# DeltaNet mixer: instructions of other engines' results emitted one or more parts later, values first in the chunk stage, and a new layout of the slots

## The chip, the cores and the metric

The kernel runs on one core of one Trainium2 chip. The metric is the device time of one execution in microseconds (us). The core has engines that run side by side, each with its own in-order queue: TensorE (PE; its weight loads are shown as PEld), VectorE (DVE), ScalarE (ACT), GpSimd (POOL) and SyncE (SP), which issues most DMA transfers.

## The reference, cut to what matters

The program is one step of a two-layer network on 128 context and 512 latent tokens of width 1024: a gated DeltaNet mixer, a feed-forward block, a Hyena convolution mixer, a second feed-forward block. The change touches the DeltaNet mixer alone. It has 8 heads with keys and values of 128; tokens are cut into chunks of 64, ten for a head, and each direction (forward, backward) scans its chunks in order:

```python
def step(s, xs):
    w_c, u_c, qd_c, aqk_c, kt_c, gl_c = xs
    v_new = u_c - jnp.einsum('bhcd,bhde->bhce', w_c, s)
    o_c = (jnp.einsum('bhcd,bhde->bhce', qd_c, s)
           + jnp.einsum('bhij,bhje->bhie', aqk_c, v_new))
    s = s * gl_c[..., None, None] + jnp.einsum('bhcd,bhce->bhde', kt_c, v_new)
    return s, o_c
```

Here `w_c` and `u_c` come from triangular systems of each chunk that do not depend on `s`. After the scan, `o` of both directions is summed, RMS-normalised (`o * rsqrt(mean(o*o) + eps)`), multiplied by a gate `silu(h @ w_gate)`, and multiplied by the output weights.

## The kernel before, in words

The mixer's function `gdn` makes one period for each h from -3 to 7. In a period seven kinds of work run for different heads: `gdn_scan(h)`, `gdn_norm(h-1)` (normalise and transpose the output), `gdn_chunks(h+1)`, `gdn_pre(h+2)`, the projections `gdn_gemm(h+3)` and their short convolutions `gdn_conv`, one or two `gdn_gate` products, and some parts of `ada`, which loads and multiplies the modulation weights (128 x 1024 pieces on SyncE's queue). In the last period `gdn_finish` splits the outputs for the output product.

Each of them is a generator whose yields cut it into parts. `weave` hands out the parts over the 30 slots (`SLOTS`) of a period: a stream (generator, n, a, b) has its n parts spread evenly from slot a to slot b; what is left is emitted at the end of the period. The tables `PERIOD`, `GATES` and `LOADS` hold a and b, with three phases for h < 0, h < 5 and the rest; `EMIT` is the order of the streams within a slot. Emission gives the priority; below it a scheduler takes from each engine's ready instructions, so that an engine's final order is near the emitted one but not equal to it.

`gdn_scan` has ten steps for a head, eight on latent chunks in a chain and two on context chunks. One step, for both directions: TensorE multiplies q and k by the state (line 1373, tile `ps_s`), VectorE makes `y` from it with the values `vyz` (L1378), TensorE multiplies by the chunk matrix `lt` (L1384, L1386 where there is no state), ScalarE evicts that to `w` or `od` (L1392), TensorE multiplies by the keys (L1407), VectorE makes the next state `s` (L1413). GpSimd adds the two directions to `o` (L1398), and ScalarE squares a finished token block (L1403, tile `junk`).

`gdn_pre` makes the squared norms (`gdn_norms`: transposes `ps_kq`, squares on ScalarE L1159, then VectorE L1161), the products `ps_kk` and from them `fa` (L1212); writes `fa` to DRAM (`ft`, L1219) and reads its diagonal blocks back as `ln` (L1226), both issued by ScalarE; VectorE negates `ln` to `bn` (L1232, L1233) and inverts small blocks; the result goes through DRAM (`bd`) to the tiles `tm` and `tt`. `gdn_chunks` multiplies these to the chunk matrices: `ps_c` (L1297), `ps_aq` (L1302), three rounds of `ps_y` (L1320) into `lt`, and last transposes the values (`ps_vt`, L1336), which ScalarE evicts in ten pieces to `vyz` (L1341). `ps_vt`, `ps_c`, `ps_aq` and `ps_y` share two PSUM buffers.

Projections, gates and the feed-forward products use three matmuls for one, on high and low parts (`wh`, `wl`, `xh`, `xl`; lines 146 and 134).

Of the kernel before, what the change touches and what calls it, by code (L numbers as in the profile page):

```python
# [35 lines left out]

SLOTS = 30
PERIOD = dict(
    scan=(0, SLOTS),
    norm=(11, 21),  # L40
    pre=((2, 21), (1, 25), (4, 25)),
    chunks=((7, 30), (1, 25), (3, 20)),
    gemm=((2, 8, 14), (0, 10, 20), (22, 0, 11)),
    gemm_len=(8, 7, 10),
    finish=(27, 30),
)
GEMM_ORDER = (1, 0, 2)

GATES = (
    (5, 15, 25),  # L50
    (-3, 17, 20),
    (6, 16, 24),
    (4, 5, 14),
    (4, 13, 28),
    (3, 23, 30),
    (7, 27, 30),
    (7, 3, 15),
)

LOADS = (  # L60
    (0, 0, 28),
    (3, 10, 26),
    (0, 5, 30),
    (10, 3, 26),
    (3, 1, 22),
    (1, 7, 29),
    (3, 6, 30),
    (6, 0, 26),
    (13, 0, 21),
    (18, 0, 24),  # L70
    (11, 5, 30),
)

EMIT = ['scan', 'loads', 'norm', 'conv', 'chunks', 'pre', 'gemm', 'finish', 'gate']
MOD_PARTS = (4, 5, 4, 1, 1, 0, 1, 3, 4)
# [15 lines left out]
class _Kernel:  # L91
# [780 lines left out]
    def gdn(self, xs):  # L872
        nc, A, V, G, PE, I = self.nc, self.A, self.V, self.G, self.PE, self.I
        W = I["gdn_w_in"][0]
        with ExitStack() as st:
# [78 lines left out]
            for h in range(-3, H):  # L954
# [10 lines left out]
                if 0 <= h + 2 < H:  # L965
                    add("pre", self.gdn_pre(h + 2, hd[h + 2]), 18, PERIOD["pre"][ph])
                if 0 <= h + 1 < H:
                    add("chunks", self.gdn_chunks(h + 1, hd[h + 1]), 11, PERIOD["chunks"][ph])
                if 0 <= h + 3 < H:
# [168 lines left out]
    def gdn_norms(self, h, hd):  # L1138
# [7 lines left out]
        for t0, tn in ((0, 2), (2, 2), (4, 1)):  # L1146
            ps = self.pg.tile([128, 512], F32, tag="g", name="ps_kq")
            for n in range(2 * tn):
                t, c = t0 + n // 2, n % 2
                self.PE.transpose(ps[:, n * 128 : n * 128 + 128], qk[:, t, c * 128 : c * 128 + 128],  # L1150
                                  self.ident)
            for c in range(2):
                rs = slice(64 * c, 64 * c + 64)
                A.copy(kz[rs, t0 : t0 + tn, c, :],
                       ps.rearrange("p (t c d) -> p t c d", t=2, c=2)[rs, :tn, c, :])
            for n in range(2 * tn):
                t, c = t0 + n // 2, n % 2
                j = p.tile([128, 128], F32, tag="junk", name="junk")
                A.activation(j, ps[:, n * 128 : n * 128 + 128], AF.Square, accum_out=ss[:, c, t : t + 1])  # L1159
            yield  # L1160
        V.tensor_scalar(out=ss, in0=ss, scalar1=EPS, scalar2=None, op0=ALU.add)  # L1161

# [22 lines left out]
    def gdn_pre(self, h, hd):  # L1185
# [38 lines left out]
        for d in range(2):  # L1224
            src = ft[d * 41600 : (d + 1) * 41600].rearrange("(l x) -> l x", x=1040)[:, :1024]
            nc.scalar.dma_start(ln[64 * d : 64 * d + 40],  # L1226
                                src.rearrange("l (j i) -> l j i", i=64)[:, :, :16])
        yield
        zz, bn = self.zz, self.bn
# [54 lines left out]
    def gdn_chunks(self, h, hd):  # L1284
# [3 lines left out]
        lt = self.lt[h % 2]  # L1288
        fa, tm, tt, rinv, vt = hd["fa"], hd["tm"], hd["tt"], hd["rinv"], hd["vt"]


        for d in range(2):
# [8 lines left out]
            for t in range(NT):  # L1301
                PE.matmul(pa[:, t * 64 : t * 64 + 64], tm[:, d, t, :], fa[:, d, t, 1, :],  # L1302
                          start=True, stop=True)
            view = lambda x: x[:, :320].rearrange("p (t i) -> p t i", t=NT)
            V.tensor_mul(tm[:, d].rearrange("p t (c i) -> p t c i", c=2), _bc(view(pc), 2, 2),
# [6 lines left out]
        for k in range(3):  # L1312
            cur = y if k else tt
            for ds, ts in ((slice(0, 1), slice(0, 4)), (slice(1, 2), slice(0, 4)),
# [16 lines left out]
                yield  # L1331
        vy = self.vyz[h % 2]
        for t0, tn in ((0, 4), (4, 1)):
            pv = pm.tile([128, 512], F32, tag="m", name="ps_vt")
            for t in range(t0, t0 + tn):
                PE.transpose(pv[:, (t - t0) * 128 : (t - t0 + 1) * 128],  # L1336
                             vt[:, t * 128 : (t + 1) * 128], ident)
            for t in range(t0, t0 + tn):
                for c in range(2):
                    rs = slice(64 * c, 64 * c + 64)  # L1340
                    A.activation(vy[rs, t, c, :], pv[rs, (t - t0) * 128 : (t - t0 + 1) * 128], AF.Copy,  # L1341
                                 scale=rinv[rs, c, t : t + 1])
        yield
        hd["vy"] = vy

    def gdn_scan(self, h, hd):
# [7 lines left out]
        seen = {}  # L1354
        state = {}
        for d in range(2):
            s = p.tile([128, 128], F32, tag=f"s1{d}", name="s", bufs=2)
            nc.sync.dma_start(s, self.I["state_delta"][0, 0, d, h])
            state[1, d] = s
# [5 lines left out]
        for pair in steps:  # L1365
# [21 lines left out]
            for seq, d, t, c, rs, ro in pair:  # L1387
# [4 lines left out]
                A.activation(w, pss[d][:, 128:256], AF.Copy, scale=kt[:, c, d, t : t + 1])  # L1392
                seen[t, c] = seen.get((t, c), 0) + 1
            yield
            for seq, d, t, c, rs, ro in pair:
# [3 lines left out]
            for t in {x[2] for x in pair}:  # L1399
                if seen.get((t, 0), 0) + seen.get((t, 1), 0) == 6:  # L1400
                    seen[t, 0] += 1
                    j = p.tile([128, 128], F32, tag="junk", name="junk")
                    A.activation(j, o[:, t, :], AF.Square, accum_out=oss[:, t : t + 1])  # L1403
            if pair[0][:4] == (1, 0, 4, 1):
# [3 lines left out]
            for seq, d, t, c, rs, ro in pair:  # L1408
# [8 lines left out]
                state[seq, d] = s2  # L1417
            yield
        for d in range(2):
            nc.sync.dma_start(self.O[2][0, 0, d, h], state[0, d])  # L1420
# [429 lines left out]
```

## Time and profile before

| | |
|---|---|
| median of 3 runs (lowest to highest) | 2046.1 us (2042.37 to 2047.77) |
| the profiled execution | 2051.41 us, its span 2049.6 us |
| busy in the span: PE, PEld | 1967.1 us (96%), 1818.0 us (89%) |
| busy in the span: DVE, ACT, POOL | 1498.7 us (73%), 949.3 us (46%), 135.5 us (7%) |
| matmuls, DVE and ACT instructions | 13259, 3175, 2185 |
| scans of heads 0 to 7 | from about 270 us to 725 us |

A span of an engine is the time in which at least one of its instructions runs; matmuls are pipelined and overlap, so that a busy PE is not one at its peak. The clock column gives the granted TensorE clock as a share of 2.4 GHz; its lower level is 0.5 (1.2 GHz). The scans of the heads follow each other: head 2 from 376.7 us, head 3 from 431.1, head 4 from 491.1, head 5 from 563.5, head 6 from 621.8, head 7 from 688.0 to 724.9.

### The profile page before, as it was taken

How to read it: one execution, taken by the hardware profiler on the slowest of the kernel's cores; microseconds unless marked ns; L12 is line 12 of the kernel's file. 1: busy time of each engine (PE TensorE's matmuls, PEld its weight loads, DVE VectorE, ACT ScalarE, POOL GpSimd, SP SyncE). 2: the span in 40 equal slices, each digit the busy share in tenths (PEclk: the TensorE clock that was granted, in tenths of full speed). 3: DMA queues.
4: the chain of work that ended last, by engine and by line, in shares of the span. 5: the costliest groups of instructions: out<-in, count | busy, mean ns of one | idle time of the engine just before them, and what ended most of it. 6: DMA issues, size and time to landing. Idle time of an engine off the chain costs nothing.

```text
span 2049.6 us, 34532 instructions
## 1 busy us (share of the span) xinstructions
PE 1967.1 (96%) x13259; PEld 1818.0 (89%) x13259; DVE 1498.7 (73%) x3175; ACT 949.3 (46%) x2185; POOL 135.5 (7%) x241
## 2 busy tenths in 40 slices
PE   7998999999999999999999999999999999999997
PEld 4676888988865789999999998999979999999997
DVE  6887787886663469956956867787787985785674
ACT  4466456655343466533533534333337652452442
POOL 0132011121100100000000000111000000000000
PEclk8999999999998999999999999999999999999999
DMA  7765445343455652223222244222353232232221
GB/s 241 261 203 150 130 113 144 80 116 108 137 167 168 212 181 79 84 74 91 83 73 85 69 129 127 69 88 83 116 172 110 82 92 73 76 92 73 83 59 56
DMA packets 344836, 237.01 MB, mean 116 GB/s; under 512 B 62274, under 2 KB 314810, under 8 KB 344671
## 3 DMA queue, kind: packets, MB, share of 16 engines
q1 hardware_dynamic: 322495, 230.18, 37.6%
q10 hardware_dynamic: 22176, 4.62, 1.1%
q8 instruction: 104, 1.70, 0.3%
q14 instruction: 61, 0.50, 0.1%
HBM read 202.57 MB, written 32.19 MB: 115 GB/s over the span
## 4 chain that ended last, share of the span: by engine, by line
PE 76%; DVE 10%; DMA 5%; ACT 4%; issue 2%; POOL 1%; ACTq 0%; POOLq 0%; DVEq 0%; SPq 0%
PE ps_d L134 15%; PE ps_g L456 11%; PE ps_u L456 11%; PE ps_hp L146 8%; PE ps_o L134 5%; PE ps_gu L456 4%; PE ps_p L146 3%; PE ps_ab L1626 2%; PE ps_ada L212 2%; PE ps_g L1683 2%; DVE cacc L1127 1%; PE ps_gate L146 1%; DMA ln<-ft 1%; PE ps_s L1407 1%; PE ps_y L1320 1%
## 5 line engine op out<-in xcount | busy, mean ns | idle before, releaser
L121 ACT CAST wh<-raw 128x512 fp32r<-128x512 f32 (+2 forms) x241 | 179.0, 763 | 278.0 <-PE ps_d L134 168.3
L122 DVE TENSOR_TENSOR wl<-raw,wh 128x512 fp32r<-128x512 f32 (+2 forms) x241 | 206.8, 873 | 35.5 <-ACT wh L121 34.5
L134 PE MATMUL ps_d<-xh,wh 128*128 128x320 f32 x688 | 212.9, 310 | 3.9 <-ACT wh L121 3.9
L134 PE MATMUL ps_d<-xl,wh 128*128 128x320 f32 x688 | 212.9, 310 | 0.0
L134 PE MATMUL ps_d<-xh,wl 128*128 128x320 f32 x688 | 211.9, 309 | 0.0
L421 ACT CAST ph<-ws 128x512 fp32r<-128x512 f32 x176 | 109.1, 621 | 138.8 <-PE ps_g L456 41.7
L456 PE MATMUL ps_u<-qh,ph 128*128 128x322 f32 x528 | 164.9, 312 | 1.4 <-ACT ps_g L470 1.4
L456 PE MATMUL ps_u<-ql,ph 128*128 128x322 f32 x528 | 165.5, 313 | 0.0
L456 PE MATMUL ps_u<-qh,pl 128*128 128x322 f32 x528 | 163.8, 310 | 0.0
L422 DVE TENSOR_TENSOR pl<-ws,ph 128x512 fp32r<-128x512 f32 x176 | 120.6, 689 | 38.1 <-ACT ph L421 37.6
L572 DVE SCALAR_TENSOR_TENSOR x<-ps_d,ng,x 128x128 f32<-128x128 f32 x144 | 58.7, 435 | 108.9 <-PE ps_d L134 108.9
L134 PEld LDWEIGHTS ps_d<-xh,wh 128*128 128x128 f32 x688 | 129.2, 188 | 5.5 <-ACT wh L121 5.0
L146 PE MATMUL ps_p<-xh,wh 128*128 128x320 f32 x384 | 128.8, 335 | 1.8 <-ACT junk L1159 1.0
L134 PEld LDWEIGHTS ps_d<-xl,wh 128*128 128x128 f32 x688 | 129.2, 188 | 0.8 <-DVE xl L561 0.7
L134 PEld LDWEIGHTS ps_d<-xh,wl 128*128 128x128 f32 x688 | 129.3, 188 | 0.0
L146 PE MATMUL ps_hp<-xh,wh 128*128 128x320 f32 (+1 forms) x384 | 123.6, 323 | 0.7 <-DVE xp L1574 0.7
L146 PE MATMUL ps_p<-xh,wl 128*128 128x320 f32 x384 | 123.0, 320 | 0.0
L146 PE MATMUL ps_p<-xl,wh 128*128 128x320 f32 x384 | 122.8, 320 | 0.0
L146 PE MATMUL ps_hp<-xh,wl 128*128 128x322 f32 (+1 forms) x384 | 120.1, 313 | 0.0
L146 PE MATMUL ps_hp<-xl,wh 128*128 128x320 f32 (+1 forms) x384 | 119.7, 312 | 0.0
L456 PE MATMUL ps_g<-qh,wh 128*128 128x322 f32 x352 | 109.6, 311 | 2.5 <-ACT ps_u L463 2.5
L456 PE MATMUL ps_g<-ql,wh 128*128 128x322 f32 x352 | 110.1, 313 | 0.0
(418 smaller groups left out, 5681.6 us busy)
## 6 DMA issues: line engine op xcount, KB each, us to landing
raw<-in_ada_w_dram SPq DMA_DIRECT2D x96, 512.0 KB
raw<-in_ffn_w_gu_dram SPq DMA_DIRECT2D x88, 512.0 KB
raw<-in_gdn_w_in_dram SPq DMA_DIRECT2D x33, 512.0 KB
raw<-in_ffn_w_down_dram SPq DMA_DIRECT2D x32, 512.0 KB
raw<-in_hy_w_in_dram SPq DMA_DIRECT2D x24, 512.0 KB
h_lat<-hlo SPq DMA_DIRECT2D x16, 512.0 KB
hs<-h_lat SPq DMA_DIRECT2D x32, 256.0 KB
raw<-in_ffn_w_down_dram SPq DMA_DIRECT2D x16, 384.0 KB
```

The costliest lines, as they stand in the source:

```text
L121: self.A.copy(wh[:, ks, :], v[:, ks])
L122: self.V.tensor_sub(wl[:, ks, :], v[:, ks], wh[:, ks, :])
L134: self.PE.matmul(ps, a[:, k, :], b[:, sl], start=(n == 0), stop=(n == 3 * nk - 1))
L146: self.PE.matmul(ps, a[:, k, :], b[:, sl], start=(n == 0), stop=(n == 3 * nk - 1))
L212: PE.matmul(ps[32 * j : 32 * j + 32, :], self.sc[:, k, :], loaded[j * 512 // n][:, c : c + 512], start=(k == 0), stop=(k == KD - 1), skip_ ...
L421: A.copy(h, src)
L422: V.tensor_sub(l, src, h)
L456: self.PE.matmul(ps[:, :322], a[:, k, :], b, start=start and n == 0, stop=n == 11, skip_group_check=True)
L572: V.scalar_tensor_tensor(out=x[d][:, sl], in0=p1[:, pl], scalar=gate[:, c, d : d + 1], in1=x[d][:, sl], op0=ALU.mult, op1=ALU.add)
L1127: V.scalar_tensor_tensor(out=acc[:, c:e], in0=xp[:, k + c : k + e], scalar=wc, in1=acc[:, c:e], op0=ALU.mult, op1=ALU.add)
L1626: PE.matmul(ps, a_[:, m, it, js], b_[it], start=(c == 0), stop=(c == 5))
L1683: PE.matmul(pv[:, gi * 256 : gi * 256 + 256], a_[:, e, cs], b_[:, m, jt, :], start=(c == 0), stop=(c == 11))
```

## The change

The same instructions are emitted, in another order; on each engine their number by line and shape is the same. (1) In `gdn_pre` seven yields (`TRAVEL`) instead of one stand between the load of `ln` and its first reader, and the stream counts 25 parts instead of 18. (2) In `gdn_norms` one yield more stands before VectorE reads the squares. (3) In `gdn_chunks` the transposes and evictions of the values come first instead of last, a yield stands between `ps_c` with `ps_aq` and VectorE's product of `ps_c`, and the stream counts 16 parts instead of 11. (4) In `gdn_scan` the square of a finished block is kept in a list and emitted after the next step's evictions. (5) All slot tables and `EMIT` have new numbers.

```diff
 PERIOD = dict(
     scan=(0, SLOTS),
-    norm=(11, 21),
-    pre=((2, 21), (1, 25), (4, 25)),
-    chunks=((7, 30), (1, 25), (3, 20)),
-    gemm=((2, 8, 14), (0, 10, 20), (22, 0, 11)),
-    gemm_len=(8, 7, 10),
-    finish=(27, 30),
+    norm=(12, 21),
+    pre=((2, 17), (0, 24), (0, 28)),
+    chunks=((7, 29), (3, 21), (3, 20)),
+    gemm=((1, 10, 14), (0, 10, 21), (21, 4, 16)),
+    gemm_len=(3, 7, 4),
+    finish=(26, 27),
 )
 GATES = (
...
-    (4, 5, 14),
+    (2, 12, 13),
...
-    (7, 3, 15),
+    (6, 6, 12),
 )
 LOADS = (
...
-    (13, 0, 21),
+    (16, 1, 21),
...
-    (11, 5, 30),
+    (8, 9, 30),
 )
-EMIT = ['scan', 'loads', 'norm', 'conv', 'chunks', 'pre', 'gemm', 'finish', 'gate']
+EMIT = ['loads', 'finish', 'pre', 'scan', 'conv', 'gemm', 'norm', 'gate', 'chunks']
...
-                    add("pre", self.gdn_pre(h + 2, hd[h + 2]), 18, PERIOD["pre"][ph])
+                    add("pre", self.gdn_pre(h + 2, hd[h + 2]), 18 + TRAVEL, PERIOD["pre"][ph])
-                    add("chunks", self.gdn_chunks(h + 1, hd[h + 1]), 11, PERIOD["chunks"][ph])
+                    add("chunks", self.gdn_chunks(h + 1, hd[h + 1]), 16, PERIOD["chunks"][ph])
...
             yield
+        yield
         V.tensor_scalar(out=ss, in0=ss, scalar1=EPS, scalar2=None, op0=ALU.add)
...
-        yield
+        for _ in range(TRAVEL):
+            yield
         zz, bn = self.zz, self.bn
...
+        vy = self.vyz[h % 2]
+        for t0, tn in ((0, 4), (4, 1)):
+            pv = pm.tile([128, 512], F32, tag="m", name="ps_vt")
+            for t in range(t0, t0 + tn):
+                PE.transpose(pv[:, (t - t0) * 128 : (t - t0 + 1) * 128],
+                             vt[:, t * 128 : (t + 1) * 128], ident)
+            for t in range(t0, t0 + tn):
+                for c in range(2):
+                    rs = slice(64 * c, 64 * c + 64)
+                    A.activation(vy[rs, t, c, :], pv[rs, (t - t0) * 128 : (t - t0 + 1) * 128], AF.Copy,
+                                 scale=rinv[rs, c, t : t + 1])
+        hd["vy"] = vy
+        yield
         for d in range(2):
...
+            yield
             view = lambda x: x[:, :320].rearrange("p (t i) -> p t i", t=NT)
...
-        vy = self.vyz[h % 2]
-        for t0, tn in ((0, 4), (4, 1)):
-            pv = pm.tile([128, 512], F32, tag="m", name="ps_vt")
...
-        yield
-        hd["vy"] = vy
...
+        ripe = []
+        def squares(n):
+            while len(ripe) > n:
+                t = ripe.pop(0)
+                j = p.tile([128, 128], F32, tag="junk", name="junk")
+                A.activation(j, o[:, t, :], AF.Square, accum_out=oss[:, t : t + 1])
...
                 seen[t, c] = seen.get((t, c), 0) + 1
+            squares(0)
             yield
...
-                    A.activation(j, o[:, t, :], AF.Square, accum_out=oss[:, t : t + 1])
+                    ripe.append(t)
...
             yield
+        squares(0)
```

In the changed kernel the line numbers are 2 to 14 higher, and the values' eviction has L1303, their transpose L1298, the square L1367. Three places of the order follow, before and after.

VectorE, period 5: from the products `fa` of the last head (7) to its first reader of `ln`, before:

```order
L1212 TENSOR_TENSOR fa<-ps_kk,X 128x128 x2
L1413 SCALAR_TENSOR_TENSOR s<-s,egl,ps_s 128x128 x2
L1326 TENSOR_TENSOR fa<-tt,ps_y_6752 128x512
L1378 SCALAR_TENSOR_TENSOR y<-ps_s,sy,vyz 128x128 x2
L1326 TENSOR_TENSOR fa<-tt,ps_y_6784 128x512
L1326 TENSOR_TENSOR fa<-tt,ps_y_6822 128x2x128
L1456 TENSOR_TENSOR oT<-oT,gg 128x640
L1413 SCALAR_TENSOR_TENSOR s<-s,egl,ps_s 128x128 x2
L1378 SCALAR_TENSOR_TENSOR y<-ps_s,sy,vyz 128x128 x2
L1330 TENSOR_TENSOR lt<-tt,ps_y_6864 64x4x128
L1232 TENSOR_SCALAR bn<-ln 40x256
```

The same after; the row of `fa` is two rows above the first one here:

```order
L1426 SCALAR_TENSOR_TENSOR s<-s,egl,ps_s 128x128 x2
L228 TENSOR_TENSOR mod_73<-ps_adat,cols_a 128x16 x2
L1391 SCALAR_TENSOR_TENSOR y<-ps_s,sy,vyz 128x128 x2
L1323 TENSOR_TENSOR tm<-ps_c,kg 128x640
L124 TENSOR_TENSOR wl<-raw,wh 128x512
L239 SCALAR_TENSOR_TENSOR acol_8036<-mod_73,cols_a 128x16
L1344 TENSOR_TENSOR fa<-tt,ps_y_6701 128x512
L1426 SCALAR_TENSOR_TENSOR s<-s,egl,ps_s 128x128 x2
L124 TENSOR_TENSOR wl<-raw,wh 128x512
L1391 SCALAR_TENSOR_TENSOR y<-ps_s,sy,vyz 128x128 x2
L1344 TENSOR_TENSOR fa<-tt,ps_y_6733 128x512
L1236 TENSOR_SCALAR bn<-ln 40x256
```

Between `fa` and the reader of `ln` stand 9 rows before and 12 after; the scan's rows `s` and `y` are two pairs of each in both.

ScalarE at the seam from the scan of head 5 to that of head 6, before (the `vyz` are head 6's):

```order
L1403 ACTIVATE junk,oss<-o 128x128
L1341 ACTIVATE vyz<-ps_vt,rinv 64x128
L1403 ACTIVATE junk,oss<-o 128x128
L1341 ACTIVATE vyz<-ps_vt,rinv 64x128 x8
L1392 ACTIVATE od<-ps_s,kt 128x128
L1434 ACTIVATE o<-o,of 128x128 x5
L1392 ACTIVATE od<-ps_s,kt 128x128
```

The same seam after (the `vyz` are head 7's; head 6's stand in the period before):

```order
L1405 ACTIVATE w<-ps_s,kt 128x128 x2
L1303 ACTIVATE vyz<-ps_vt,rinv 64x128 x2
L1405 ACTIVATE w<-ps_s,kt 128x128
L1303 ACTIVATE vyz<-ps_vt,rinv 64x128 x3
L1405 ACTIVATE w<-ps_s,kt 128x128
L1303 ACTIVATE vyz<-ps_vt,rinv 64x128 x2
L1367 ACTIVATE junk,oss<-o 128x128
L1303 ACTIVATE vyz<-ps_vt,rinv 64x128
L1367 ACTIVATE junk,oss<-o 128x128
L1303 ACTIVATE vyz<-ps_vt,rinv 64x128 x2
L1327 COPY tt<-ps_aq 64x5x64 x2
L1448 ACTIVATE o<-o,of 128x128 x5
```

Before, eight pieces stand in a row ahead of the scan's first `od`; after, pieces in twos and threes stand between the last `w` of head 5.

TensorE in the next to last step of head 2's scan, from the state's product (L1373) to the product with `lt` (L1384), before:

```order
L1373 MATMUL ps_s<-s,qk 128x128
L146 MATMUL ps_p<-xh_1273,wl 128x320
L1320 MATMUL ps_y_4770<-fa,tm 128x128 x4
L146 MATMUL ps_p<-xh_1081,wh 128x320
L146 MATMUL ps_p<-xl_1082,wh 128x320
L146 MATMUL ps_p<-xh_1081,wl 128x320
L146 MATMUL ps_p<-xh_1180,wh 128x320
L1320 MATMUL ps_y_4777<-fa,tm 128x128 x2
L1384 MATMUL ps_s<-y,lt 128x128
```

After, from the first state's product (now L1386) of such a step at the end of head 2's scan to the keys' product (now L1420), with L1397 for L1384:

```order
L1386 MATMUL ps_s<-s,qk 128x128
L148 MATMUL ps_p<-xl_1266,wh 128x320
L1386 MATMUL ps_s<-s,qk 128x128
L148 MATMUL ps_p<-xh_1265,wl 128x320
L148 MATMUL ps_p<-xh_1273,wh 128x320
L1397 MATMUL ps_s<-y,lt 128x128
L148 MATMUL ps_p<-xl_1274,wh 128x320
L1397 MATMUL ps_s<-y,lt 128x128
L148 MATMUL ps_p<-xh_1273,wl 128x320
L1420 MATMUL ps_s<-w,ktok 128x128
L1298 MATMUL ps_vt<-ident,vt 128x128 x5
L1420 MATMUL ps_s<-w,ktok 128x128
```

Before, seven rows of other work stand in that link; after, two stand in it and one or two in the next.

## Rows read from the trace of the kernel before

**Rows 1.** Windows, scans of heads 2, 5, 6, 7: length, busy by engine, clock, DMA.

```profile
376.70:431.10 54.40, 53.57 (x439) 48.81 (x440) 45.03 (x124) 29.95 (x100) 10.86 (x23) 1.00 0.31 82
...
563.50:621.80 58.30, 53.66 (x405) 39.59 (x405) 37.41 (x115) 25.91 (x89) 7.03 (x12) 0.97 0.55 162
...
621.80:688.00 66.20, 61.78 (x362) 43.16 (x361) 24.57 (x67) 23.03 (x69) 4.83 (x11) 0.85 0.62 201
...
688.00:724.90 36.90, 36.79 (x243) 28.71 (x243) 18.23 (x54) 17.86 (x53) 6.45 (x11) 1.00 0.67 197
```

**Rows 2.** Windows of heads 2, 5, 6, 7, modulation matmuls alone.

```profile
376.70:431.10 54.40, 2.11 (x10) 0.29 (x10) 0.00 (x0) 1.00 0.31 82
...
563.50:621.80 58.30, 12.77 (x65) 1.78 (x64) 0.59 (x1) 0.97 0.55 162
...
621.80:688.00 66.20, 16.47 (x54) 2.10 (x54) 0.59 (x1) 0.85 0.62 201
...
688.00:724.90 36.90, 7.38 (x32) 1.02 (x32) 0.59 (x1) 1.00 0.67 197
```

**Rows 3.** Waits, 176 to 746 us: who waited for whom, total, times, longest.

```profile
ACT junk L1403 <- POOL o L1398: 28.8, 20, 2.7
...
PEld ps_s L1407 <- ACT od L1392: 6.9, 10, 1.7
...
DVE y L1378 <- ACT vyz L1341: 6.5, 6, 1.5
...
DVE bn L1233 <- DMA ln<-ft: 5.6, 5, 2.2
...
PEld ps_s L1407 <- ACT w L1392: 3.0, 12, 0.8
...
DVE bn L1232 <- DMA ln<-ft: 2.8, 3, 1.2
```

**Rows 4.** Timeline, 604 to 609 us: start, duration, engine, line [idle before].

```profile
604.20 0.28 DVE L1232 TENSOR_SCALAR bn<-ln 40x256 f32<-40x256 f32 x1 [1.16 <-DMA ln<-ft]
...
604.37 0.30 PE L146 MATMUL ps_gate<-xh,wh 128*128 128x320 f32 x1
...
604.52 0.30 PE L146 MATMUL ps_gate<-xl,wh 128*128 128x320 f32 x1
...
606.69 0.37 DVE L1233 TENSOR_SCALAR bn<-ln 40x256 f32<-40x256 f32 x1 [2.21 <-DMA ln<-ft]
...
608.51 0.49 PE L1373 MATMUL ps_s<-s,qk 128*128 128x128 f32 x2 [3.69 <-DVE s L1413]
```

**Rows 5.** Windows around the two stalls: columns as in rows 1.

```profile
608.00:612.00 4.00, 3.49 (x18) 3.50 (x19) 3.51 (x17) 0.92 (x3) 0.91 (x2) 0.71 0.00 0
...
612.00:616.00 4.00, 4.00 (x30) 3.91 (x29) 3.25 (x8) 1.42 (x6) 0.20 (x1) 0.87 0.16 63
...
624.00:628.00 4.00, 1.90 (x16) 1.34 (x18) 1.88 (x11) 3.89 (x12) 0.00 (x0) 0.84 0.97 273
...
627.30:647.20 19.90, 19.49 (x88) 13.66 (x88) 3.65 (x8) 4.82 (x14) 0.00 (x0) 0.50 0.45 161
```

**Rows 6.** Timeline, 623 to 627 us, ScalarE and TensorE.

```profile
623.59 3.01 ACT L1341 ACTIVATE vyz<-ps_vt,rinv 64x128 f32<-64x128 f32 x8
...
624.40 0.49 PE L1384 MATMUL ps_s<-y,lt 128*128 128x128 f32 x2 [1.28 <-DVE y L1378]
...
626.62 0.37 ACT L1392 ACTIVATE od<-ps_s,kt 128x128 f32<-128x128 f32 x1
```

**Rows 7.** Timeline, 435 to 437 us, seam to head 3.

```profile
435.78 0.80 PE L1297 MATMUL ps_c<-tm,fa 64*64 64x64 f32 x20 [0.89 <-ACT vyz L1341]
...
436.52 0.35 DVE L1378 SCALAR_TENSOR_TENSOR y<-ps_s,sy,vyz 128x128 f32<-128x128 f32 x1 [1.34 <-ACT vyz L1341]
```

**Rows 8.** Timeline, 715 to 719 us, one scan step of head 7.

```profile
714.97 0.61 PE L1373 MATMUL ps_s<-s,qk 128*128 128x128 f32 x4
...
718.23 0.65 PE L1373 MATMUL ps_s<-s,qk 128*128 128x128 f32 x4
```

More of the change, by code (lines that the diff above doesn't have):

```diff
@@ L37 @@
 SLOTS = 30
+TRAVEL = 7
 PERIOD = dict(
     scan=(0, SLOTS),
-    norm=(11, 21),
-    pre=((2, 21), (1, 25), (4, 25)),
-    chunks=((7, 30), (1, 25), (3, 20)),
-    gemm=((2, 8, 14), (0, 10, 20), (22, 0, 11)),
-    gemm_len=(8, 7, 10),
-    finish=(27, 30),
+    norm=(12, 21),
[4 more added lines that the diff above has]
+    finish=(26, 27),
 )
@@ L49 @@
 GATES = (
-    (5, 15, 25),
-    (-3, 17, 20),
-    (6, 16, 24),
-    (4, 5, 14),
-    (4, 13, 28),
-    (3, 23, 30),
-    (7, 27, 30),
-    (7, 3, 15),
+    (5, 11, 27),
+    (-3, 18, 20),
+    (6, 14, 30),
+    (2, 12, 13),
+    (4, 15, 29),
+    (3, 29, 30),
+    (7, 25, 30),
+    (6, 6, 12),
 )
 LOADS = (
[L61 to L68, printed above, removed]
-    (13, 0, 21),
-    (18, 0, 24),
-    (11, 5, 30),
+    (0, 0, 25),
+    (4, 6, 30),
+    (0, 9, 30),
+    (10, 2, 25),
+    (3, 8, 19),
+    (1, 0, 26),
+    (2, 2, 25),
+    (6, 3, 26),
+    (16, 1, 21),
+    (18, 0, 25),
+    (8, 9, 30),
 )
-EMIT = ['scan', 'loads', 'norm', 'conv', 'chunks', 'pre', 'gemm', 'finish', 'gate']
+EMIT = ['loads', 'finish', 'pre', 'scan', 'conv', 'gemm', 'norm', 'gate', 'chunks']
 MOD_PARTS = (4, 5, 4, 1, 1, 0, 1, 3, 4)
@@ L1331, in gdn_chunks @@
                 yield
-        vy = self.vyz[h % 2]
-        for t0, tn in ((0, 4), (4, 1)):
-            pv = pm.tile([128, 512], F32, tag="m", name="ps_vt")
[L1335 to L1342, printed above, removed]
-        yield
-        hd["vy"] = vy
     def gdn_scan(self, h, hd):
@@ L1401, in gdn_scan @@
                     seen[t, 0] += 1
-                    j = p.tile([128, 128], F32, tag="junk", name="junk")
-                    A.activation(j, o[:, t, :], AF.Square, accum_out=oss[:, t : t + 1])
+                    ripe.append(t)
             if pair[0][:4] == (1, 0, 4, 1):
```

## Prediction

> **What bounds the kernel now.** I began with the busy time by stretch, one stretch for each head's scan, since the change touches only the loop over heads. In [rows 1] the matmul columns are nearly full everywhere, but those spans overlap. The weight loads are the better measure of what the array is fed. Their idle time, the stretch less their busy time, is 5.6 us for head 2, 18.7 for head 5, 23.0 for head 6 and 8.2 for head 7. Part of that is no idleness: the modulation matmuls stream long after a short weight load. Taking their matmul time less their weight-load time off [rows 2], there remain 5.6 - 1.8 = 3.8 us (head 2), 18.7 - 11.0 = 7.7 (head 5) and 23.0 - 14.4 = 8.6 (head 6); these are lower bounds, since the modulation spans overlap others. So TensorE bounds heads 0 to 4 with a few us lost in each, and in heads 5 and 6, where there are no projections left to fill in, the scan's chain from TensorE to VectorE to TensorE to ScalarE and back sets the time. I then looked for what ends the waits [rows 3] and followed the two largest on the timeline.
>
> First, at 604.52 us TensorE starts a gate matmul and then nothing until 608.51 [rows 4]. It needs the new state s from VectorE, and that stands in VectorE's queue behind two negations which wait 1.16 and 2.21 us for the table `ln` to land. Just after it the granted clock is 0.71 and 0.87 [rows 5], so part of the time it is at 1.2 GHz. Second, at the seam from head 5 to 6, ScalarE evicts eight pieces of `vyz` in a row from 623.59 for 3.01 us; TensorE waits 1.28 us for y, which waited for `vyz`, and the scan's own eviction of `od` starts only at 626.62 [rows 6]. The stretch from 624 holds 1.90 us of matmul in 4, and then the clock is 0.50 for 19.9 us [rows 5].
>
> **The change part by part.** No instruction is added or taken away; every gain or loss is a wait.
>
> *(a) TRAVEL.* The first reader of `ln` is emitted seven parts after its load instead of one. In [rows 4] the gap is 608.51 - 604.52 = 3.99 us; two matmuls of that kind start 0.15 us apart, so 3.8 us were lost. At half clock were (1 - 0.71) x 4 / 0.5 = 2.3 and (1 - 0.87) x 4 / 0.5 = 1.0 us, 3.4 in all; with the loads busy for 7.4 of those 8 us it cost half of that by 7.4/8, 1.6 us. Together 5.3 us. The other waits for `ln` are 5.6 + 2.8 - 3.4 = 5.0 us of VectorE [rows 3], and what TensorE lost by them lies between 0 and 5.0. But the order of VectorE for the last head has two scan steps between `fa` and `ln` before, and two after: more rows, not more steps. The transfer itself is unchanged. I take -4, bounds -10.3 and 0.
>
> *(b) Values first in the chunk stage, at the seam of head 6.* The ten evictions of head 6's `vyz` no longer stand between its chunk stage and its scan: y of the first step finds them ready. Lost were 4.00 - 1.90 = 2.1 us, and the half clock over 19.9 us with loads busy for 13.66, which at 2.4 GHz would have been 6.8 us less if nothing else held the scan: 8.9 us. What moves in: head 7's `vyz` now stand at the same seam, but between the last evictions of scan 5, in twos and threes. A wait for an eviction is then one to three pieces long instead of eight. I take -7, bounds -8.9 and 0.
>
> By the Trainium skill (TensorE: Matmul & The Clock Gate, section HAM oscillation — how this bites in real kernels) the penalty is the throttled time by the share of the clock that is lost, here half: 10.0 us instead of my 6.8. The rows show loads busy for only two thirds of that stretch, so I keep mine; by the rule the sum would be 3 us lower.
>
> *(c) The same at the five other seams.* At the seam to head 3 TensorE waits 0.89 us for `vyz` and y 1.34 [rows 7]. All such waits of y come to 6.5 us [rows 3]. One us a seam: -5, bounds -6.5 and 0.
>
> *(d) Squares later.* ScalarE idles 28.8 us in 20 waits for GpSimd's sums [rows 3]. It is not the bound; what TensorE loses is the late eviction behind the square. All of TensorE's weight loads that wait for `od` or `w` lose 6.9 + 3.0 = 9.9 us [rows 3]. The 20 squares stand before at most 20 of 160 evictions, an eighth, though before the later ones: I take twice that share, -2, bounds -9.9 and 0.
>
> *(e) The new slots, at the end of a scan.* One step of three links takes 718.23 - 714.97 = 3.26 us [rows 8], 1.09 each, of which two pairs of matmuls fill about 0.4; the other 0.65 us needs four or five rows of projection at 0.15. In the order a link at the end of head 2's scan had seven such rows and now has one or two. About five such links in each of five heads lack 0.25 us on average, 6 us, where before about half as much was lacking: +3, bounds 0 and +12.
>
> *(f) The new slots, work moved between heads.* Gate 3 (48 matmuls at 0.15, 7.2 us) goes from head 4's period to head 2's; gate 7 goes from head 7's to head 6's; three modulation parts more stand in period 5 and three fewer in 7. Where the scan's chain is the limit the filler is free; where TensorE is, it costs its full time. Above head 2's 3.8 us, heads 5 and 6 idle for 3.9 + 4.8 = 8.7 us, of which (a) and (b) already use 3.8 + 2.1; 2.8 are left. Head 7 idles 8.2 - 6.4 = 1.8 us or more [rows 2]; it is nearly full, so that one gate less may shorten it or bare the chain. -2, bounds one gate either way, -7 and +7. The extra yields after the norms and between `ps_c` and `ps_aq` I cost at nothing: they move a VectorE product behind work that TensorE has queued there, and uncovered would cost the 1 us of one link.
>
> A second rule bears on what is left to gain. By the Trainium skill (Trainium Kernel Development and Optimization, Best Practices) matmul busy time is a poor measure of headroom and weight-load busy time a good one. By matmul busy, head 6's stretch would hold 4.4 us to gain in all, and (b) with (f) could not exceed that; [rows 1] has 23.0 by weight loads, so the trace sides with the rule.
>
> The sum is -4 - 7 - 5 - 2 + 3 - 2 = -17 us. The profiled execution took 2051.4 us (span 2049.6 and 1.8 around it), so 2034.4 for such a one. It lies 5.3 us above the median of the runs, 2046.1; the same 17 us off that median give 2029.
>
> **The rivals.**
> 1. *The clumps only move: no change.* For it: the order still has ten `vyz` in a row in two other places, the same eviction work, and for the last head as many scan steps before `ln`. Against it: y waits for none of them. With (b), (c) and (f) at nothing: 2046.1 - 4 - 2 + 3 = 2043.
> 2. *Starved scan ends: slower.* In periods 0 to 6 the chunk stage ends by slot 21 and the preparation by 24 or 28, so the last steps stand alone with what is left of the projections. If each of the 25 links waits 1.0 us instead of 0.25, that is 25 us, and five stretches at half clock as after [rows 4] lose 1.6 each, 8 us; against the 20 us of gains: 2059. It decides from 0.8 us a link. For it: the thin rows in the order. Against it: in head 7 of before, links as thin run at 1.09 us.
> 3. *The loop levels out: twice the gain.* With (a), (b) and (c) at their good ends, 5 us from the squares and 4 from the moved work, no loss at the ends: 10.3 + 8.9 + 6.5 + 5 + 4 = 35, 2011. For it: head 2 shows that a head can run with 3.8 us idle. Against it: head 5 keeps its slow transfers.
> That the yields do nothing because a scheduler reorders is excluded: `vyz` now stands a whole scan ahead of its user.
>
> **How the numbers follow.** A difference of 0.3%, 2040.0 to 2052.2, is about what this measurement can tell from none. The sum 0.48, rival 3 0.22, rival 1 0.18, rival 2 0.12. Faster is the sum and rival 3, 0.70; same 0.18; slower 0.12. All bounds at their good ends give 2046.1 - 42.6 = 2003.5, at their bad ends 2046.1 + 19 = 2065. The range leaves out most of rival 2: 2003 to 2050; the likeliest alone, 2015 to 2040.
>
> **What the profile after would show.** Right: no TensorE gap near 4 us behind a `bn` negation; waits of y for `vyz` near zero, ScalarE's for GpSimd's sums well under 28.8; the stretch at clock 0.50 in head 6 gone; weight-load idle of heads 5 and 6 several us lower. Wrong: (a), if `bn` still waits 2 us; (b), if the clock falls again in period 6; (e), if the last links idle by a us each. A loss in period 7 of over 5 us would make (f) wrong, and a loss before 237 us, where the preparation of head 0 has nothing beside it, would be one that I have not counted.

## The result and the profile after

The changed kernel takes 2017.0 us (median of 4 runs, 2014.7 to 2017.8) against 2045.2 us (4 runs, 2042.4 to 2047.8): a ratio of 0.9861, 95% interval 0.9844 to 0.9878, 28 us faster. The forecast was 2029, with 2015 to 2040 for its own sum.

The profiled execution after took 2014.7 us, its span 2012.9. It is the lowest of its runs and that of before lies 5 to 6 us above its median, so the two traces differ by 36.7 us, some 8 more than the medians. In the first part of the profile page after, the weight loads are busy for about as long as before (1810.7 us against 1818.0) and the matmuls for 17 us less; so 29 of the 36.7 us are time between weight loads:

```profile
PE 1949.9 (97%) x13259; PEld 1810.7 (90%) x13259; DVE 1501.7 (75%) x3175; ACT 946.4 (47%) x2185; POOL 136.3 (7%) x241
```

The next table is worked out from the traces: the first `ps_s` matmul of head 1, the lengths from each head's first `ps_s` to the next one's, and the length from head 7's to the first `ps_d` matmul, in us (one execution of each kernel; the experiments are told below). `ps_d` is the down product of the feed-forward block behind the mixer; the expectation of e10 calls that point the output product, but the mixer's output product, `ps_o`, starts some 170 to 180 us earlier.

| kernel | head 1 starts | 1 | 2 | 3 | 4 | 5 | 6 | 7 to `ps_d` | `ps_d` starts |
|---|---|---|---|---|---|---|---|---|---|
| before | 316.7 | 60.0 | 54.4 | 60.0 | 72.4 | 58.3 | 66.2 | 207.8 | 895.8 |
| after | 313.9 | 58.8 | 56.4 | 59.6 | 62.5 | 60.0 | 49.7 | 199.1 | 860.0 |
| e1, code alone | 315.9 | 58.0 | 59.6 | 53.6 | 69.9 | 63.1 | 48.9 | 206.6 | 875.6 |
| e9, gates and loads alone | 312.7 | 61.4 | 61.1 | 57.1 | 65.0 | 64.1 | 51.1 | 199.9 | 872.4 |
| e11, values first alone | 317.5 | 60.2 | 57.9 | 62.4 | 72.3 | 60.3 | 52.7 | 207.2 | 890.5 |
| e10, after with the old gates | 316.2 | 60.5 | 59.8 | 55.4 | 69.9 | 60.6 | 45.3 | 205.2 | 872.9 |
| e6, after with the old gates and loads | 321.4 | 62.0 | 57.3 | 59.1 | 69.3 | 60.4 | 50.9 | 208.1 | 888.5 |
| e12, after with gate 4 early | 318.3 | 63.7 | 57.3 | 59.7 | 64.7 | 56.8 | 51.0 | 200.7 | 872.2 |

Of the 36.7 us, 35.8 were gained up to that point: 9.9 in head 4, 16.5 in head 6, 8.7 behind the start of head 7, 2.8 before head 1; heads 2 and 5, which got more filler, are 2 us longer each. The windows of heads 2, 5, 6 and 7 after, against [rows 1]:

```profile
372.70:429.10 56.40, 56.17 (x477) 52.76 (x476) 44.53 (x114) 29.14 (x94) 8.44 (x17) 1.00 0.41 109
551.20:611.20 60.00, 58.44 (x473) 41.15 (x472) 40.40 (x125) 30.53 (x109) 6.43 (x14) 0.99 0.81 246
611.20:660.90 49.70, 49.70 (x351) 39.82 (x349) 21.55 (x55) 15.95 (x50) 4.55 (x10) 0.94 0.65 218
660.90:691.40 30.50, 30.50 (x212) 26.91 (x212) 22.01 (x58) 19.15 (x52) 4.16 (x8) 1.00 0.83 245
```

Weight-load idle fell from 23.0 to 9.9 us in head 6 and from 8.2 to 3.6 in head 7; in head 5 it is 18.9 as before, but the modulation matmuls there [rows 2] grew from 65 to 83 and take 16.74 - 2.44 = 14.3 us of it:

```profile
551.20:611.20 60.00, 16.74 (x83) 2.44 (x82) 0.60 (x1) 0.99 0.81 246
```

Head 4's window, before and then after: the gate that left it is 48 of the 55 matmuls by which x550 became x495, and the length went down by 9.9 us, more than the gate's 7.2.

```profile
491.10:563.50 72.40, 68.70 (x550) 62.66 (x549) 45.80 (x123) 33.83 (x109) 7.54 (x18) 1.00 0.46 133
```

```profile
488.70:551.20 62.50, 60.31 (x495) 54.77 (x494) 42.45 (x118) 30.61 (x102) 8.75 (x14) 1.00 0.46 130
```

The waits after, 176 to 746 us, that answer to [rows 3]; a wait of y for `vyz` has no row any more, and the wait of 2.9 us for `ln` in the last row stands at 245 us, ahead of head 1's scan:

```profile
ACT junk L1367 <- POOL o L1412: 19.7, 17, 3.5
...
PEld ps_s L1420 <- ACT w L1405: 4.8, 10, 1.6
...
PEld ps_s L1420 <- ACT od L1405: 4.4, 10, 1.6
...
DVE bn L1236 <- DMA ln<-ft: 4.1, 2, 2.9
```

The timeline at the last head's two negations, against [rows 4]: they wait 1.18 us and nothing, and the longest gap between two starts on TensorE near them is 0.52 us (it was 3.99).

```profile
578.07 0.28 DVE L1236 TENSOR_SCALAR bn<-ln 40x256 f32<-40x256 f32 x1 [1.18 <-DMA ln<-ft]
...
580.13 0.37 DVE L1237 TENSOR_SCALAR bn<-ln 40x256 f32<-40x256 f32 x1
```

And the windows of the seam to head 6 after, against [rows 5]. The clock still falls, to 0.56 and 0.59, but comes back within 7 us instead of 20; the 20 us that follow hold 17.58 us of weight loads:

```profile
610.00:614.00 4.00, 3.87 (x34) 3.75 (x34) 1.11 (x6) 1.65 (x6) 0.00 (x0) 0.56 0.91 343
614.00:618.00 4.00, 4.00 (x17) 2.23 (x17) 1.22 (x3) 2.00 (x5) 0.00 (x0) 0.59 0.04 15
618.00:638.00 20.00, 20.00 (x154) 17.58 (x153) 9.57 (x26) 7.19 (x21) 0.91 (x2) 1.00 0.59 187
```

So nearly everything that the prediction wanted to see is there (not the shorter idle time of head 5), and so are two of its signs of being wrong: `bn` still waits over 2 us once, and the clock falls again at the seam to head 6. That does not show that the named waits were the gain, and the runs say that most of it was elsewhere.

### The profile page after: what moved, and what is told of

It reads as the page before. It is cut to its first block, busy times and chain, and to the rows that moved or that the text cites. A ratio compares the mean times of both kernels' runs of the same rounds, so it can differ in the third digit from the quotient of the medians.

```text
span 2012.9 us, 34509 instructions
## 1 busy us (share of the span) xinstructions
PE 1949.9 (97%) x13259; PEld 1810.7 (90%) x13259; DVE 1501.7 (75%) x3175; ACT 946.4 (47%) x2185; POOL 136.3 (7%) x241
## 4 chain that ended last, share of the span: by engine, by line
PE 70%; DVE 2%; ACT 2%; DMA 1%; issue 0%; POOL 0%; ACTq 0%; POOLq 0%; SPq 0%; DVEq 0%
PE ps_d L136 15%; PE ps_g L458 11%; PE ps_u L458 11%; PE ps_hp L148 8%; PE ps_o L136 5%; PE ps_gu L458 4%; PE ps_ab L1640 2%; PE ps_g L1697 2%; PE ps_ada L214 2%; PE ps_gate L148 2%; PE ps_y L1338 1%; PE ps_p L148 1%; PE ps_s L1420 1%; PE ps_s L1386 1%; PE ps_s L1397 1%; ACT wh L123 0%
```

## The experiments

Each has its ratio to the kernel before, with a 95% interval; a difference of two ratios by 2045 us gives the us, uncertain by about 5 where two intervals meet.

**e1 and e2: code alone, tables alone.** e1 has the changed code with `PERIOD`, `GATES`, `LOADS` and `EMIT` of before; e2 the reverse.

```diff
# e1, against the changed kernel
-    chunks=((7, 29), (3, 21), (3, 20)),
+    chunks=((7, 30), (1, 25), (3, 20)),
... (and every other number of the four tables)
```

> The four edits of the code (TRAVEL, values first, squares later, the yields) with the slot tables and the emission order of before. Theory (the sum of the prediction: waits taken away by the code, terms a to d, -18 us, tables about 0): 2027 us, ratio 0.991; the 1.16 and 2.21 us waits of VectorE for the loaded diagonal blocks and the long half-clock stretch in head 6 are gone, gate 3 still lengthens head 4's stretch to some 72 us. Rival (the tables do it: work moved between heads, -9.9 in head 4's stretch, -16.5 in head 6's): at most 5 us gained, 2040 us or more, ratio 0.997 to 1.00, and head 6's stretch stays above 62 us.

> The new slot tables, gates, loads and emission order with the code of before. Theory (terms e and f, about +1, with up to -10 from the moved gates): 2036 to 2047 us, ratio 0.995 to 1.00, with the waits for the diagonal blocks and for the values still there. Rival (the tables do most): 2018 to 2026 us, ratio 0.987 to 0.991, head 4's stretch near 62 us and head 6's near 50. If the gains of code alone and tables alone do not add up to the 28 us of both, the two need each other.

Measured: e1 2031.8 us, 0.9942 (0.9921 to 0.9962), -12 us. e2 2033.1 us, 0.9945 (0.9923 to 0.9966), -11 us. Neither theory nor rival: the code brought two thirds of the 18 us, the tables 11 instead of about none, and head 6's stretch shrank to 49 us in both. The two add to 23 of the 28 us.

**e9 and e11: one part alone on the kernel before.** e9 has only the new `GATES` and `LOADS`; e11 only the values first.

```diff
# e9, against the kernel before
-    (4, 5, 14),
+    (2, 12, 13),
-    (7, 3, 15),
+    (6, 6, 12),
-    (13, 0, 21),
+    (16, 1, 21),
... (and the other rows of GATES and LOADS)
# e11, against the kernel before: the block of ps_vt and vyz moved up
+        vy = self.vyz[h % 2]
+        for t0, tn in ((0, 4), (4, 1)):
...
         for d in range(2):
...
-        vy = self.vyz[h % 2]
-        for t0, tn in ((0, 4), (4, 1)):
```

> The kernel before with the new tables of gates and modulation loads alone; code, period table and emission order of before. Theory (term f by itself was sized ten times too small: putting these two tables back cost the changed kernel 24 us): 2020 to 2026 us, ratio 0.988 to 0.991, head 4's stretch near 63 us. Rival (they bring little by themselves and need the rest of the change, since both kinds of edits fill the same idle time): 2035 us or more, ratio 0.995 or more, with the waits for the diagonal blocks and for the values as long as before.

> The kernel before with the values first in the chunk stage, and nothing else. Theory (terms b and c as the prediction has them): 12 us faster than before, ratio 0.994, no half-clock stretch of 20 us in head 6, no waits of y for the values. Rival (code alone brought 12 us in all, of which TRAVEL has a part): 5 to 8 us faster, ratio 0.996 to 0.9975. Second rival (the emptied seams fill with other waits, and the fitted tables no longer fit): no faster than before, ratio 0.999 or more.

Measured: e9 2028.4 us, 0.9917 (0.9903 to 0.9931), -17 us. e11 2044.5 us, 1.0001 (0.9991 to 1.0012), nothing. The theory of e9 is missed by 2 us; that of e11 falls, and its second rival (no faster) is what was measured. And e9 keeps the waits that the prediction priced:

```profile
DVE y L1378 <- ACT vyz L1341: 6.3, 5, 2.3
DVE bn L1232 <- DMA ln<-ft: 5.4, 4, 2.1
...
DVE bn L1233 <- DMA ln<-ft: 2.4, 2, 1.3
```

They come to 14.1 us, 14.9 before. In e11 no wait of y for the values is left, and head 6 is as the prediction wanted it (52.7 us at clock 1.00 instead of 66.2 at 0.85):

```profile
377.70:435.60 57.90, 56.23 (x438) 50.70 (x437) 44.23 (x123) 29.54 (x94) 8.93 (x21) 0.96 0.30 77
630.60:683.30 52.70, 50.51 (x357) 36.50 (x356) 24.14 (x67) 19.43 (x61) 4.82 (x11) 1.00 0.72 237
```

Of the 13.5 us gained there it lost most at other places: heads 2, 3 and 5 are 3.5, 2.4 and 2.0 us longer. The 5 us that remain up to `ps_d` are about what the profiled execution before lies above its median. The timeline of the seam to head 2 in e11 shows how. TensorE stands for 4 us before a projection, not for `vyz` but for the evictions and squares of `ps_kq`, which shares the PSUM buffers of `ps_p`:

```profile
372.31 0.61 PE L1333 MATMUL ps_y<-fa,tm 128*128 128x128 f32 x4
...
376.38 0.28 ACT L1159 ACTIVATE junk<-ps_kq 128x128 f32<-128x128 f32 x1
...
376.80 0.64 PE L146 MATMUL ps_p<-xh,wh 128*128 128x320 f32 x1 [3.88 <-ACT junk L1159]
```

In the trace before, the evictions of `vyz` stand at this place and the work on `ps_kq` behind them. So at this seam, with the first clump of ScalarE's work taken out, the next stands in the scan's way; the seams to heads 3 and 5 were not followed. The other stall of before, behind the negations, is there too, 4.3 us between two starts (609.62 and 613.93):

```profile
609.62 0.31 PE L146 MATMUL ps_gate<-xh,wl 128*128 128x320 f32 x1
612.62 0.37 DVE L1233 TENSOR_SCALAR bn<-ln 40x256 f32<-40x256 f32 x1 [3.56 <-DMA ln<-ft]
...
613.93 1.23 PE L1373 MATMUL ps_s<-s,qk 128*128 128x128 f32 x4 [4.00 <-DVE s L1413]
```

**e6 and e10: the changed kernel with the old gates and loads, and with the old gates alone.**

```diff
# e10, against the changed kernel (e6 has the old LOADS as well)
-    (2, 12, 13),
+    (4, 5, 14),
-    (6, 6, 12),
+    (7, 3, 15),
... (and the other rows of GATES)
```

> The changed kernel with the old tables of gates and modulation loads (gate 3 in period 4, gate 7 in period 7, 3 modulation parts fewer in period 5), the other tables as changed. Theory (term f, from the traces: head 4's stretch lost 9.9 us with the gate and the tail after the last scan got 8.7 us shorter): 5 to 10 us slower than the changed kernel, ratio 0.9885 to 0.991; head 4's stretch is back at 69 us or more and head 2's at 53 or less. Rival (work moved between full heads costs the same wherever it stands): within 2 us, ratio 0.985 to 0.987, with head 2 as much shorter as head 4 is longer. Second rival (fitted tables): 8 us or more, with the loss in other heads than 2, 4 and 7.

> The changed kernel with the old table of gates alone; the modulation loads stay as changed. It parts the 24 us of the two tables. Theory (the gates carry the work of 7 us each, moved from the full head 4 to head 2 and from the last head to head 6): 12 to 20 us slower than the changed kernel, ratio 0.992 to 0.996, head 4's stretch near 69 us, and the stretch from head 7's scan to the output product 5 us or more longer. Rival (the modulation parts carry it: three parts more of period 5): within 5 us of the changed kernel, ratio 0.986 to 0.9885.

Measured: e6 2041.4 us, 0.9978 (0.9968 to 0.9989), 24 us slower than the changed kernel, more than twice the theory's; its losses are before head 1 (7.5 us), in head 1 (3.2) and 4 (6.8) and behind the start of head 7 (9.0). e10 2028.4 us, 0.9919 (0.9904 to 0.9934), 12 us slower, the low end of its theory. So without them almost nothing of the change is left, and gates and loads have about half each. In e10's windows of heads 2 and 4, head 4 got its gate back and is 7.4 us longer, as a full head should be; head 2 lost its gate and is 3.4 us longer too:

```profile
376.70:436.50 59.80, 56.10 (x444) 51.94 (x443) 45.93 (x123) 31.09 (x104) 10.80 (x21) 0.94 0.34 89
491.90:561.80 69.90, 67.57 (x543) 61.83 (x541) 45.97 (x122) 33.45 (x110) 7.26 (x17) 1.00 0.51 146
```

Its weight-load idle is 59.8 - 51.9 = 7.9 us, against 56.4 - 52.8 = 3.6 with the gate. The timeline of the end of head 2's scan in e10 shows the place: the projections have run out, TensorE has nothing but the scan's own links, and one late eviction of `w` (behind two of `vyz`, a conversion and a convolution piece on ScalarE) leaves it empty for 2.25 us.

```profile
422.60 1.05 PE L1386 MATMUL ps_s<-s,qk 128*128 128x128 f32 x4 [0.47 <-DVE s L1426]
423.53 0.49 PE L1397 MATMUL ps_s<-y,lt 128*128 128x128 f32 x2
426.27 0.49 PE L1420 MATMUL ps_s<-w,ktok 128*128 128x128 f32 x2 [2.25 <-ACT w L1405]
```

The window behind it has the clock at 0.64:

```profile
427.00:436.50 9.50, 8.73 (x39) 7.85 (x40) 6.04 (x19) 5.86 (x21) 2.58 (x6) 0.64 1.07 309
```

In the changed kernel gate 3 runs from 390 to 401 us in this head, the projections come later for it, and from 414 to 423 us they fill every link. But head 2 is not shorter for the gate alone. Without it, 21 more projection matmuls run in head 2 (152 against 131) and 21 fewer in head 3 (126 against 147), whose stretch is 4.2 us shorter. Heads 2 and 3 together take 115.2 us without the gate and 116.0 with it: its 7.2 us of matmuls cost 0.8 (e6, also without it, has 116.4; these are single executions). With the old code they cost more: e9 has the gate there too, and the two heads grew from 114.4 to 118.2 us, by 3.8, while head 4 gave back 7.4 in both kernels.

With gate 7 back in its period, in e10, the part behind the start of head 7 is 6.1 us longer (31 gate and 10 modulation matmuls more stand there), and head 6 only 4.4 shorter without it. The timelines of the last gate matmul and the first output product, in the changed kernel and then in e10, show what the last period gains: the output product starts directly behind the gate, in the changed kernel 12 us ahead of the last `ps_s` matmul (at 692.0 us), in e10 1 us behind it (699.5). All fourteen traces have one of these two pictures, by the period of gate 7.

```profile
680.04 0.31 PE L148 MATMUL ps_gate<-xh,wl 128*128 128x320 f32 x1
680.19 0.30 PE L136 MATMUL ps_o<-xh,wh 128*128 128x320 f32 x1
```

```profile
700.31 0.31 PE L148 MATMUL ps_gate<-xh,wl 128*128 128x320 f32 x1
700.46 0.30 PE L136 MATMUL ps_o<-xh,wh 128*128 128x320 f32 x1
```

**e3: values last in the changed kernel.**

```diff
-        vy = self.vyz[h % 2]
-        for t0, tn in ((0, 4), (4, 1)):
...
         for d in range(2):
...
                 yield
+        vy = self.vyz[h % 2]
+        for t0, tn in ((0, 4), (4, 1)):
```

> The changed kernel with the transposes and evictions of the values put back to the end of the chunk stage, all else as changed. Theory (terms b and c): 7 to 12 us slower than the changed kernel, 2024 to 2029 us, ratio 0.990 to 0.992, with waits of y for the values at the seams and a half-clock stretch in head 6. Rival (the new slots end the chunk stage early enough, so that where the values stand no longer matters): within 3 us of the changed kernel, ratio 0.985 to 0.988.

Measured: 2027.0 us, 0.9916 (0.9898 to 0.9935), 11 us slower. The size is the theory's; its signs are not there: no wait of y for the values, and 3.4 us at half clock at the seam to head 6. The loss is spread: the start of head 1 is 7 us later, head 2 4.6 us longer, head 5 2.0.

**e4 and e8: TRAVEL 1 and 10 in the changed kernel.**

```diff
-TRAVEL = 7
+TRAVEL = 1
```

> The changed kernel with TRAVEL = 1: one yield between the load of the diagonal blocks and its first reader, the stream counted as 19 parts. Theory (term a): 4 us slower than the changed kernel (0 to 10), about 2021 us, ratio 0.988, with a wait of 1 to 2 us of the negation in head 5's or 6's stretch. Rival (the wait went by the new slots of the preparation, not by the seven parts): within 1.5 us of the changed kernel, ratio 0.9855 to 0.987. Second rival (the seven parts only spread the rest of the preparation thinner and that costs): 2 to 5 us faster than the changed kernel.

> The changed kernel with TRAVEL = 10, 28 parts in the stream. Theory (the seven parts already cover the load): within 2 us of the changed kernel, ratio 0.985 to 0.987, and the waits of the negation for the load not above the 4.1 us of the changed kernel. Rival 1 (the load is still not covered): 1 to 4 us faster, 0.984 to 0.9855. Rival 2 (fitted tables): 5 us slower or more, ratio 0.9885 or more, with no wait for the load to show for it.

Measured: e4 2025.2 us, 0.9907 (0.9886 to 0.9928), 9 us slower; e8 2021.3 us, 0.9888 (0.9871 to 0.9905), 6 slower. The waits for `ln` in e4, and then in e8:

```profile
DVE bn L1237 <- DMA ln<-ft: 2.6, 3, 1.5
...
DVE bn L1236 <- DMA ln<-ft: 1.6, 3, 0.8
```

```profile
DVE bn L1236 <- DMA ln<-ft: 5.8, 1, 5.8
```

Together 4.2 us with one yield, 4.1 with seven, 5.8 with ten, but not at the same places. With seven and ten yields 2.9 and 5.8 us of it are one wait at 245 and 249 us, ahead of head 1's scan, and heads 1 to 4 have none; with one yield 2.8 us stand in the scans of heads 0 to 2. So the yields do take the waits out of those scans, and lengthen the one ahead of them. That this is the gain is not shown: what TRAVEL = 1 loses stands before head 1 (3.3 us) and in heads 2 and 5 (3.9 and 4.9 us longer), head 5 has no wait for `ln` in e4, where the theory put one, and near the longest one, 1.55 us in head 2 at 403 us, TensorE has no gap over 0.6 us. The cause is open.

**e5: squares at once.**

```diff
                     ripe.append(t)
+                    squares(0)
```

> The changed kernel with each square emitted at once again, as before, all else as changed. Theory (term d, and the sums so far: values last costs 11 and TRAVEL = 1 costs 9, together already more than the 16 that all the code edits are worth with the new tables): 0 to 3 us slower than the changed kernel, ratio 0.986 to 0.9875; ScalarE's waits for GpSimd's sums go back from 19.7 to about 25 to 29 us, with TensorE not late for it. Rival (the tables were fitted to this very code, and any change of the order costs some 8 to 10 us by the way the instructions then happen to fall): 8 us slower or more, ratio 0.990 or more.

Measured: 2016.3 us, 0.9867 (0.9847 to 0.9887): no difference from the changed kernel. ScalarE's waits for the sums do not go back to the 25 to 29 us of the theory either:

```profile
ACT junk L1367 <- POOL o L1412: 19.6, 17, 3.5
```

**e7: one number moved by one slot.**

```diff
-    norm=(12, 21),
+    norm=(13, 22),
```

> The changed kernel with one number moved by one slot: the normalisation of the head before stands in slots 13 to 22 instead of 12 to 21. No term of the prediction speaks of it. Theory (single waits make the time): within 2 us of the changed kernel, ratio 0.985 to 0.987. Rival (fitted tables, any change of the order costs): 5 us slower or more, ratio 0.9885 or more; then the 8 to 11 us of the values and of TRAVEL are in part no more than that.

Measured: 2019.6 us, 0.9884 (0.9863 to 0.9905), 5 us slower, uncertain by 5. It is no proof of either side, but with e8 it suggests that a shift that no term speaks of can cost some 5 us here. Of the 9 to 11 us of e3 and e4 as much may be no more than that.

**e12: gate 4 early, a try at a faster version.**

```diff
-    (4, 15, 29),
+    (0, 12, 20),
```

> The changed kernel with gate 4 moved from period 4, slots 15 to 29, to period 0, slots 12 to 20. Where the runs point: filler is worth most where the scan leaves idle time, and in the changed trace weight loads leave 3 to 4 us free at 255 to 270 us, in head 0's scan, while head 4's stretch is full. Theory: head 4's stretch some 6 us shorter, the stretch before head 1 3 to 6 us longer, 0 to 4 us faster than the changed kernel in all, ratio 0.984 to 0.986. Rival (fitted tables: any change of the order costs 3 to 4 us, as one slot of the normalisation did): 2 to 6 us slower, ratio 0.987 to 0.989.

Measured: 2026.1 us, 0.9900 (0.9885 to 0.9915), 8 us slower than the changed kernel, more than theory and rival have. Head 1 starts 4.4 us later and head 1's stretch is 4.9 longer, but head 4, which lost the 48 matmuls of its gate, did not get shorter. Its window, and then its modulation matmuls alone:

```profile
499.00:563.70 64.70, 62.16 (x498) 51.33 (x498) 44.76 (x120) 33.07 (x111) 7.44 (x15) 1.00 0.54 159
```

```profile
499.00:563.70 64.70, 9.50 (x44) 1.32 (x44) 0.00 (x0) 1.00 0.54 159
```

Other work took the gate's place: x498 is no fewer than the x495 of the changed kernel. 44 modulation matmuls stand in this stretch instead of 26, and they came from head 5, which has 64 instead of 82 and is 3.2 us shorter. So this run does not tell what head 4 would take with less to do.

Weight-load idle in the window is 13.4 us instead of 7.7, matmul idle 2.5 instead of 2.2. By the Trainium skill (Trainium Kernel Development and Optimization, Best Practices) the distance to the roofline is judged by the share of peak arithmetic that is reached and by weight-load busy time, not by matmul busy time. The trace agrees in part only, for here the weight loads mislead too: 4.6 of the 5.6 us more of idle time are modulation matmuls, which stream for 9.5 us on 1.3 us of weight loads (4.2 on 0.6 in the changed kernel's head 4).

No version that was run beats the changed kernel.

## Why the prediction was right in its time and wrong in its terms

- **(a) TRAVEL, -4.** Undone in the changed kernel it costs 9 (4 to 15), in size within the bounds (its own terms, 3.8 and 1.6, add to 5.4 and not 5.3). The 3.99 us gap is gone. But it is also gone in e9, which has one yield (the longest gap on TensorE near the last negations is 0.97 us there), and e4, with one yield, has no wait for `ln` near the last negations and no more of it in all than the changed kernel. That the named mechanism was the gain is not shown.
- **(b) and (c) values first, -7 and -5.** This step failed as it was put: "y of the first step finds them ready" is so in e11, and is worth nothing there (-2 to +2 us). What the step left out, where the trace was followed, is what stands next in ScalarE's queue. In the changed kernel, with its other slots, the same edit is worth 11 (6 to 16), of which 5 may be a mere shift as in e7. Its price is no property of the wait.
- **(b), the clock.** The 20 us at half clock in head 6 are absent in every experiment, whichever edit it has (at most 10 us stand at that seam): head 6 is 45 to 55 us long in all of them. In the prediction's sum it was the property of one edit. It may not even be one of the kernel: each run's mean granted clock is on record, and the profiled execution before has 0.985, as low as any. The 44 runs of that kernel beside the experiments have 0.985 to 0.991, in the median 0.988; 0.003 of 2045 us is 6 us of full clock, so the median run stands about 12 us less at half clock than the profiled one. The nine runs at 0.990 or 0.991 took 2039 to 2045 us, the seven at 0.985 or 0.986 took 2046 to 2049; where they differ no trace shows. So a part of the 16.5 us of head 6 may belong to the profiled execution and not to the edits; the 8 us by which the traces differ more than the medians speak for it.

  By the Trainium skill (TensorE: Matmul & The Clock Gate, HAM oscillation — how this bites in real kernels) a half-clock stretch costs half its length, an estimate of 10 us for the 20. Between those two groups of runs the clock differs by 9 us of full clock and the medians by 5 us, so here about half of that rule's price shows. e11's runs have 0.990 on average, some 4 us of full clock better than before, and are no faster: what the clock gives back there is lost elsewhere.
- **(d) squares later, -2.** e5: nothing (-4 to +7 us). The squares were off the path.
- **(e) new slots, +3.** Period table and emission order with the old code cost 6 (1 to 11; e2 against e9), with the new code and old gates 7 (3 to 12; e6 against e1). The sign was right for those; with new code and new gates together it was not run, and whether starved links are what it costs was not followed. Of gaps over 0.75 us between two starts on TensorE, from 176 us to the end of head 7's scan, the changed trace has 10 (10.8 us) and that of before 27 (35.0 us); only the last links of head 1's scan lack filler.
- **(f) work moved between heads, -2, bounds -7 and +7.** This term failed in size: alone it is -17 (14 to 20), undone it is 24 (20 to 28). The step took head 2's and heads 5 and 6's idle time as a stock that a gate of 7.2 us must fit into ("above head 2's 3.8 us", "2.8 are left"). The runs show otherwise: head 4 gives back 7.4 us without the gate, and heads 2 and 3 take it for 0.8 us in the changed kernel and for 3.8 in that of before. And it gave no price to what stands behind the last gate: with gate 7 in head 6's period the output product starts 12 us ahead of the scan's end, and the part behind the start of head 7 is 6.1 us shorter. The loads, which I priced with the gates, carry half in the changed kernel; by what way no run shows.
- **The total.** -17 against -28: (b) and (c) were 12 too good as edits of the kernel before, (f) 15 too small, and the other 8 us were traced to no single edit. e1 and e9, -12 and -17, add to the whole -28, although (b) and (c), which the prediction put at 12 of the code's 18, brought nothing alone: either the code's parts need each other, or TRAVEL alone, which was not run on the kernel before, is worth more than its 4. That the time came out near was luck: two errors that cancel.
- **Rival 1** had the right reason for (b) and (c) alone, clumps that only move; rival 2's starved ends are in e10, at one place, and not in the changed kernel; of rival 3's terms, nothing was shown one by one.

Not run was the changed code with the new gates and loads on the old period table and emission order: the ratios of e1 and e9 multiply to 0.986, the changed kernel's own, so the other two tables may bring nothing.

## What to carry to other kernels

Price filler neither by its own length nor by the idle time of one stretch of one trace: 7.2 us of matmuls gave back 7.4 us in a full head, and cost 0.8 or 3.8 us in two others, by the code around them. Count what moves in where something is taken out, and compare over neighbouring stretches, since work slips over their seams. Before a wait is priced, look what stands next in the queue of the engine that it names; taking out the first clump only brought up the second. Before a stretch at half clock is priced, see by the clock of the other runs whether they have it. And where an order is laid out by hand over a dozen numbers, undo parts in both directions, from the old kernel and from the new: the same edit was worth 0 and 11 us.

## What the runs showed of the hardware that was not expected

A stall alone did not tell how long the clock stays down. Before, the longest gaps at the seam to head 6 were 1.9 and 1.3 us between two starts on TensorE, and 20 us at half clock followed [rows 5]. In e11 a stall of 4 us at 372 us left the whole of head 2 at a mean clock of 0.96, and in the changed kernel gaps of 0.8 and 1.2 us at the same seam were followed by 8 us at a mean of 0.56 and 0.59. In e10 the 2.25 us at the end of head 2's scan were followed by 9.5 us at 0.64. What else decides it no run here settles.
